# A fifth landing buffer and a reordered first block in a one-core two-block kernel

## The chip, the cores and the metric

The kernel is one program on one core of a Trainium2 chip. The metric is device time in microseconds (us), taken as the median over several executions. Before the change it was 1045.44 us, the median of 3 runs (1043.22 to 1045.67). The engines are called PE (TensorE, matrix products), ACT (ScalarE), DVE (VectorE), POOL (GpSimd) and SP (SyncE, which here only issues transfers).

## The reference

256 tokens of 1024 features pass through a first block (a modulated convolution module and a squared-ReLU network) and then through two layers of a second block (attention mixers and a gated network). The change touches only the head of the first block:

```python
mod = silu(c) @ w_mod + b_mod                  # 6 parts of 1024: sh1, s1, g1, sh2, s2, g2
h   = rms_norm(x, norm1_g) * (1 + s1) + sh1
u   = h @ w_pw1 + b_pw1                        # 1024 -> 2048
a, gate = split(u)
u   = a * sigmoid(gate)
u   = dwconv(u, w_dw) + b_dw                   # width 31, inside segments of 64 tokens
u   = silu(layer_norm(u))
x   = x + g1 * (u @ w_pw2 + b_pw2)
# then the squared-ReLU network, modulated with sh2, s2, g2
```

## The kernel before, in words

All arithmetic is float32. A weight matrix is read from memory in chunks of 128x1024, split into a rounded high part (`hi`, a copy on ACT, L409) and the remainder (`lo`, a subtraction on DVE, L426), and a product is three one-pass PE products of rounded operands (hi with high, lo with high, hi with low: L927 to L929 for the first matrix, `pw1`).

All weights come as one stream whose order is written out in `TRANSFERS`, and SP issues its transfers in that order, each of them 128x2048 (1.05 MB) or half of that. There are two kinds of landing buffers. Chunks that are split land in one of three `raw` buffers, two chunks to a buffer, which is free again once both `lo` subtractions are done. Pieces of the modulation matrix `w_mod` are used as they are and land in a `home`; of those there are four, in rotation, and one is free again when its user on PE or DVE is through (`W.used`). `Weights.pump` (L395) issues transfers until the next one has no buffer assigned. SP takes them strictly in order: when one waits for its buffer, everything behind it waits too.

In `TRANSFERS` and `PW1_STEPS` the names are these. `c0` to `c15` are the chunks of `pw1`. `F0` to `F3` are quarters of sh1 and s1, of two pieces each: PE multiplies them with silu(c) (L750), ACT copies the row of sums out (L760, into the tile `modrow`), eight small PE products turn it into columns (L777), and DVE adds the bias (L781). `M1` to `M3` mean that a quarter is taken up: the columns, and then the modulation of two of the eight feature groups (`modulated`, L864 to L873). `D0` to `D3` are pieces of s2, summed on DVE by two multiplications each (L788) with `czb`, which is silu(c) on all partitions: it is transferred (L881) and computed by a sigmoid on ACT (L979) and a multiplication on DVE (L981). `P0` to `P7` and `R0` to `R3` are pieces of g1, sh2 and g2, on PE (L750). `w0` to `w7` are the chunks of the next matrix, `pw2`.

`PW1_STEPS` sets the order in which all engines get the work of this stage. The 2048 columns of `pw1` are done as four parts q of 512 columns for two halves of the tokens, t. Chunks c0 to c11 serve q = 0 to 2 and c12 to c15 serve q = 3. When a part is complete, `glu` takes it: a sigmoid on ACT (L887) and a multiplication on DVE (L888) for each t. Then `conv` works on it: PE transforms (`x_ps`, L907), DVE multiplies by the transformed taps `wf` (L910), PE transforms back (`c_ps`, L914), ACT copies out (L919). The convolution's steps stand in the queues between the chunks. The eight PSUM banks are handed out in turn.

Ahead of `c0` the PE queue holds four products of a zeroed tile (`idle_ps`, L535), the bias products of q = 0 and 1 (L818, L819), quarter F0 (L750), the sum of squares over the features (`cs_ps`, L622), F0's columns (L777), the tap sums (`wf_ps`, L827), and the bias products of q = 2. The bias row and the tap rows lie in `rows1`, whose first half is later overwritten with `czb`.

Of the kernel before, what the change touches and what calls it, by code (L numbers as in the profile page):

```python
# [10 lines left out]
F32 = mybir.dt.float32  # L11
F32R = mybir.dt.float32r
# [3 lines left out]
P = 128  # L16
T = 256
D = 1024
# [14 lines left out]
PW2_EARLY, PW2_LATE = [0, 1, 2, 3], [4, 5, 6, 7]  # L33
WO_EARLY, WO_LATE = [6, 7, 3, 4], [5, 0, 1, 2]
EPS = 1e-6
WARM = 4
NEG = -1.0e30
VW = 392
LAYERS = 2
# [4 lines left out]


TRANSFERS = (
    "F0 c0 F1 c1,2 c3 F2 c4,5 F3 c6,7 D0 c8,9 D1 D2 c10,11 D3 P0 c12,13 P1 P2 P3 c14,15 P4 P5 w0,1 P6 P7 R0 w2,3 R1 R2 R3 "
    "w4,5,6,7"
)
PW1_STEPS = (  # L50
    "c0 F1 c1 M1 c2 F2 c3 c4 M2 c5 F3 c6 c7 M3 D0 c8 c9 D1 c10 D2 c11 D3 P0 c12 P1 c13 P2 c14 P3 c15"
)


# [423 lines left out]
def tile_conformer_then_mixer(ctx: ExitStack, tc: tile.TileContext, stream, xT, pT, vec, con, rows_in, taps, c_row, out):  # L478
    nc = tc.nc
    ctx.enter_context(tc.manual_schedule())  # L480
    cp = ctx.enter_context(tc.tile_pool(name="cp", bufs=1))
    rawp = ctx.enter_context(tc.tile_pool(name="rawp", bufs=RAWS))
    spp = ctx.enter_context(tc.tile_pool(name="spp", bufs=LOOK + 1))
    xsp = ctx.enter_context(tc.tile_pool(name="xsp", bufs=2))
    tp = ctx.enter_context(tc.tile_pool(name="tp", bufs=2))
# [4 lines left out]
    def bank(name):  # L490
        return pp_.tile([P, 512], F32, tag="b", name=name)

    vecs = cp.tile([P, NVEC], F32, name="vecs")
    cons = cp.tile([P, NCON], F32, name="cons")
    h = cp.tile([P, KB, T], F32, name="h")
# [4 lines left out]
    u = bigf[:, 2048 : 2048 + 2 * D].rearrange("p (t c) -> p t c", t=2)  # L500
    prods = bigf[:, 4096 : 4096 + NSEG * D].rearrange("p (s c) -> p s c", s=NSEG)
    wf = bigf[:, 8192 : 8192 + D]
    rows1 = bigf[:, 9216 : 9216 + 2 * D]
# [8 lines left out]
    homes = [  # L512
        cp.tile([P, 2048], F32, tag="pp", name="home0"), xsp.tile([P, 2048], F32, tag="cx", name="home1", bufs=1),
    ]
    pair = xsp.tile([P, 2, 2048], F32, tag="xs", name="home2")
    homes += [pair[:, 0, :], pair[:, 1, :]]
    W = Weights(nc, rawp, spp, stream, homes)
    W.pump()

    def V(name, i=0, n=None):  # L520
        off, cnt = VEC[name]
        return vecs[:, off + i : off + i + (n if n is not None else cnt - i)]

    def C(name):
        off, cnt = CON[name]
        return cons[:, off : off + cnt]
# [2 lines left out]
    epst = cp.tile([P, 1], F32, name="epst")  # L529
    nc.vector.memset(epst, EPS)  # L530

    nc.vector.memset(u[:, 0, :512], 0.0)
    idle_ps = bank("idle_ps")
    for _ in range(WARM):
        nc.tensor.matmul(idle_ps, u[:, 0, :P], u[:, 0, :512], start=True, stop=True)  # L535
    cz = cp.tile([P, KB, 32], F32, name="cz")
    nc.vector.memset(cz, 0.0)
    nc.scalar.preload_act_table_set("silu_and_others")
# [79 lines left out]
    def col_sum(*parts):  # L618

        ps = bank("cs_ps")  # L620
        for i, part in enumerate(parts):
            nc.tensor.matmul(ps[:, :T], ones, part, start=(i == 0), stop=(i == len(parts) - 1))  # L622
        return ps[:, :T]
# [115 lines left out]
    mods = cp.tile([P, 6, KB], F32, name="mods")  # L739
    mod_cols = bank("mod_cols")  # L740
    mod_ps = {}

    def mod_chunk(what, which, j):

        if j == 0:
            mod_ps[0] = bank("mod_ps")
        i, w = W.whole(("mod", what, which, j))
        for g in range(4):
            k = {"first": 4 * j + g, "pair": j, "one": 2 * j + g // 2}[what]
            nc.tensor.matmul(  # L750
                mod_ps[0][32 * g : 32 * g + 32, :], cz[:, k, :], w[:, 512 * g : 512 * g + 512],
                start=(j == 0), stop=(j == {"first": 1, "pair": KB - 1, "one": 3}[what]),
            )
        W.used(i)

    def mod_columns(what, which):


        row = tp.tile([P, 512], F32, tag="modrow", name="modrow", bufs=1)
        nc.scalar.copy(row, mod_ps[0])  # L760
        yield
        yield
        if what == "pair":
            at = lambda a: a.rearrange("p (q c b) -> p q c b", q=6, c=2)[:, which : which + 2]
            cols = at(mod_cols[:, :48])
            for b in range(4):
                nc.tensor.matmul(cols[:, :, :, b], row[:, b * P : (b + 1) * P], C("sel4"), start=True, stop=True)
        elif what == "one":
            at = lambda a: a.rearrange("p (q c b) -> p q c b", q=6, c=2)[:, which]
            cols = at(mod_cols[:, :48])  # L770
            for b in range(4):
                nc.tensor.matmul(cols[:, :, b], row[:, b * P : (b + 1) * P], C("sel2"), start=True, stop=True)
        else:
            at = lambda a: a.rearrange("p (q k) -> p q k", q=6)[:, :2, 2 * which : 2 * which + 2]
            cols = at(mod_cols[:, :48])
            for b in range(4):
                nc.tensor.matmul(  # L777
                    cols[:, b // 2, b % 2 : b % 2 + 1], row[:, b * P : (b + 1) * P], C("sel1"), start=True, stop=True
                )
        yield  # L780
        nc.vector.tensor_add(at(mods.rearrange("p q k -> p (q k)")), cols, at(V("b_mod")))  # L781
# [29 lines left out]
    def pw1_bias(q):  # L811

        gated[q] = [bank("g_ps") for _ in range(2)]
        kw = dict(skip_group_check=True)
        s = slice(512 * q, 512 * q + 512)
        for ps in gated[q]:
            if q < 3:
                nc.tensor.matmul(ps, ones_r, b_hi[:, s], start=True, stop=False, **kw)  # L818
                nc.tensor.matmul(ps, ones_r, b_lo[:, s], start=False, stop=False, **kw)  # L819
            else:  # L820
                nc.tensor.matmul(ps, ones[32:33, :], rows1[32:33, s], start=True, stop=False, **kw)

    def tap_sums():

        pss = [bank("wf_ps") for _ in range(2)]
        for c in range(2):
            nc.tensor.matmul(  # L827
                pss[c][:RANK], C("at")[:TAPS], rows1[:TAPS, 512 * c : 512 * c + 512], start=True, stop=True
            )
        yield  # L830
        for c in range(2):
            nc.scalar.copy(wf[:RANK, 512 * c : 512 * c + 512], pss[c][:RANK])

    for q in range(2):
        pw1_bias(q)
    sh = mods[:, 0, :]

    def quarter(c):
# [6 lines left out]
    def normed(k0, k1):  # L845
        for k in range(k0, k1):
            nc.vector.tensor_mul(xn[:, k, :], h[:, k, :], rbc)
# [4 lines left out]
    ps = col_sum(accA)  # L852
    rsqrt_(rbc, ps, 1.0 / D)
    normed(0, 2)
    for _ in work:
        pass
    sums = tap_sums()
    next(sums)
    pw1_bias(2)

    def modulated(c):

# [10 lines left out]
            nc.vector.tensor_sub(xs[:, k, T:], xn[:, k, :], xs[:, k, :T])  # L873

    modulated(0)
    for _ in sums:
        pass
    normed(2, KB)

    czb = rows1[:, :D]  # L880
    nc.sync.dma_start(czb, c_row.to_broadcast([P, D]))  # L881


    def glu(q):
# [88 lines left out]
    works = {}  # L973
    for item in PW1_STEPS.split():
        taken(item[0], int(item[1:]))
        if item == "c4":
            nc.sync.dma_start(cons[:, CON_FIRST:], con[:, CON_FIRST:])
        elif item == "c5":
            nc.scalar.activation(u[:, 0, :], czb, AF.Sigmoid)  # L979
        elif item == "c6":  # L980
            nc.vector.tensor_mul(czb, czb, u[:, 0, :])  # L981
        elif item == "c10":
            pTs0 = embedding(0)
# [31 lines left out]
        pass  # L1015
    nc.scalar.preload_act_table_set("silu_and_others")

    biasr = cp.tile([P, 5, 384], F32, name="biasr")
    rows = dram.tile([5, 384], F32, name="rows")
    skew = dram.tile([5, P + 1, 384], F32, name="skew")  # L1020

# [80 lines left out]
    ps = col_sum(*parts)  # L1102
# [8 lines left out]
    hi, lo = W.get(("pp", 0, 0))  # L1111
# [652 lines left out]
```

## Time and profile before

| | |
|---|---|
| median of 3 runs (lowest, highest) | 1045.44 us (1043.22, 1045.67) |
| the profiled execution | 1044.48 us |
| its span, first to last instruction | 1042.7 us |
| outside the span | 1.8 us |
| PE busy, share of the span | 1011.0 us, 97% |
| DVE, ACT, POOL busy | 753.6, 592.8, 101.6 us |
| mean granted PE clock | 0.978 |
| bytes moved | 192.90 MB, 185 GB/s over the span |

A line of a timeline gives the start, the time from start to end, engine, source line, operation, output and inputs by the program's names (all large work tiles are views of one tile, `big`), shape, a count where equal neighbours are merged, and in brackets the idle time of the engine before it with what ended it. `[9.31 <-DVE big L888]` says that the engine stood idle for 9.31 us until a DVE instruction of line 888 was done. A float32 product appears as several PE records. PEclk is the clock granted to PE, 1.00 being the full one.

### The profile page before, as it was taken

To read this page: it belongs to the slowest core of one execution; us is meant where nothing else is said; L and a number is where in the kernel's file an instruction comes from. 1 tells how busy PE (TensorE), PEld (TensorE's weight loads), DVE (VectorE), ACT (ScalarE), POOL (GpSimd) and SP (SyncE) were. 2 spreads that over 40 slices of the span, in tenths; PEclk is the share of its full clock that TensorE was granted. 3 is DMA by queue.
4 is the path that set the end of the run, shared out by engine and by line. 5 is a ranking of instruction groups with operands and counts; after the bars stand their busy time and mean duration, and the time that the engine had idled before them with its cause. 6 is when DMAs were issued, how large, how long until landed. Compare 5 with 4: busy or idle time off the path is not lost.

```text
span 1042.7 us, 16472 instructions
## 1 busy us (share of the span) xinstructions
PE 1011.0 (97%) x6394; PEld 870.1 (83%) x6394; DVE 753.6 (72%) x1446; ACT 592.8 (57%) x1072; POOL 101.6 (10%) x86
## 2 busy tenths in 40 slices
PE   9987989999999999999999999999999999999996
PEld 4653579888888988988888888998989888888896
DVE  5463456966878699868888865477997788886645
ACT  5522574744555554767555544674586756555455
POOL 0000022000004000002000002610000200000243
PEclk7987999999999999999999999999999999999999
DMA  9965838455554532425545555454343455555541
GB/s 376 408 235 226 338 112 267 171 202 180 186 188 160 198 125 93 162 96 188 192 174 201 177 187 195 154 172 157 107 152 122 153 197 179 199 196 174 196 162 41
DMA packets 28416, 192.90 MB, mean 185 GB/s; under 512 B 3368, under 2 KB 3757, under 8 KB 6961
## 3 DMA queue, kind: packets, MB, share of 16 engines
q1 hardware_dynamic: 26784, 188.32, 50.2%
q0 software_dynamic: 784, 1.99, 0.7%
q10 hardware_dynamic: 770, 1.54, 0.4%
q8 instruction: 50, 0.82, 0.3%
q14 instruction: 28, 0.23, 0.1%
HBM read 190.78 MB, written 2.04 MB: 185 GB/s over the span
## 4 chain that ended last, share of the span: by engine, by line
PE 78%; DVE 8%; ACT 4%; DMA 1%; issue 1%; DVEq 0%; ACTq 0%
PE g_ps L644 33%; PE g_ps L645 17%; PE g_ps L637 3%; PE mx_ps L706 3%; PE g_ps L638 2%; PE g_ps L639 2%; PE mx_ps L707 2%; PE mx_ps L708 2%; DVE lo L426 2%; DMA home<-stream 1%; ACT hi L409 1%; PE mod_ps L750 1%; PE o_ps L1423 1%; PE cs_ps L622 1%; PE pt_ps L1460 1%
## 5 line engine op out<-in xcount | busy, mean ns | idle before, releaser
L409 ACT CAST hi<-raw 128x1024 fp32r<-128x1024 f32 (+2 forms) x310 | 320.5, 1037 | 294.7 <-PE g_ps L644 148.7
L426 DVE TENSOR_TENSOR lo<-raw,hi 128x1024 fp32r<-128x1024 f32 (+2 forms) x294 | 361.0, 1231 | 125.3 <-ACT hi L409 124.4
L644 PE MATMUL g_ps<-xf,hi 128*128 128x512 f32 x704 | 247.0, 395 | 0.0
L645 PE MATMUL g_ps<-xf,lo 128*128 128x256 f32 x704 | 197.4, 280 | 0.0
L644 PEld LDWEIGHTS g_ps<-xf,hi 128*128 128x128 f32 x704 | 132.0, 187 | 30.8
L645 PEld LDWEIGHTS g_ps<-xf,lo 128*128 128x128 f32 x704 | 133.0, 189 | 0.1
L644 PE MATMUL g_ps<-big_f,hi 128*128 128x512 f32 x352 | 124.4, 397 | 0.0
L645 PE MATMUL g_ps<-big_f,lo 128*128 128x256 f32 x352 | 99.1, 281 | 0.0
L644 PE MATMUL g_ps<-big,hi 128*128 128x512 f32 x256 | 90.5, 397 | 0.0
L644 PEld LDWEIGHTS g_ps<-big_f,hi 128*128 128x128 f32 x352 | 66.1, 188 | 16.3
L645 PE MATMUL g_ps<-big,lo 128*128 128x256 f32 x256 | 72.1, 282 | 0.0
L644 PE MATMUL g_ps<-xs_h,hi 128*128 128x512 f32 x192 | 67.0, 393 | 0.0
L645 PEld LDWEIGHTS g_ps<-big_f,lo 128*128 128x128 f32 x352 | 66.4, 189 | 0.0
L644 PEld LDWEIGHTS g_ps<-big,hi 128*128 128x128 f32 x256 | 48.1, 188 | 11.8
L645 PE MATMUL g_ps<-xs_h,lo 128*128 128x256 f32 x192 | 53.8, 280 | 0.0
L608 POOL TENSOR_TENSOR accP<-accP,sq 128x256 f32<-128x256 f32 x12 | 17.8, 1480 | 331.1 <-ACT sq L607 331.1
L645 PEld LDWEIGHTS g_ps<-big,lo 128*128 128x128 f32 x256 | 48.3, 189 | 0.1
L644 PEld LDWEIGHTS g_ps<-xs_h,hi 128*128 128x128 f32 x192 | 36.0, 187 | 8.1
L637 PE MATMUL g_ps<-xs_l,hi 128*128 128x256 f32 x144 | 42.3, 294 | 0.0
L638 PE MATMUL g_ps<-xs_l,lo 128*128 128x256 f32 x144 | 41.2, 286 | 0.7 <-DVE lo L426 0.7
L637 PE MATMUL g_ps<-xn,hi 128*128 128x256 f32 x144 | 41.8, 290 | 0.0
L639 PE MATMUL g_ps<-xs_l,hi 128*128 128x256 f32 x144 | 41.0, 285 | 0.0
(363 smaller groups left out, 2238.5 us busy)
## 6 DMA issues: line engine op xcount, KB each, us to landing
raw<-stream SPq DMA_DIRECT2D x142, 1024.0 KB, 4.8
home<-stream SPq DMA_DIRECT2D x24, 1024.0 KB, 8.4
raw<-stream SPq DMA_DIRECT2D x4, 904.0 KB, 4.7
raw<-stream SPq DMA_DIRECT2D x4, 768.0 KB, 4.3
raw<-stream SPq DMA_DIRECT2D x2, 896.0 KB, 4.4
raw<-stream SPq DMA_DIRECT2D x2, 784.0 KB, 4.8
h<-xT SPq DMA_DIRECT2D x1, 1024.0 KB, 6.5
raw<-stream SPq DMA_DIRECT2D x2, 512.0 KB, 11.2
```

The lines of the kernel that those rows point to most:

```text
L409: self.nc.scalar.copy(hi[:, : PLAN[i][1]], raw)
L426: eng.tensor_sub(lo[:, :w], raw, hi[:, :w])
L608: nc.gpsimd.tensor_add(acc, acc, s)
L622: nc.tensor.matmul(ps[:, :T], ones, part, start=(i == 0), stop=(i == len(parts) - 1))
L637: nc.tensor.matmul(ps, hi, xs[:, k, :T], start=first, stop=False)
L638: nc.tensor.matmul(ps, lo, xs[:, k, :T], start=False, stop=False)
L639: nc.tensor.matmul(ps, hi, xs[:, k, T:], start=False, stop=last)
L644: nc.tensor.matmul(ps, hi, xs[:, k, :], start=first, stop=False, skip_group_check=True)
L645: nc.tensor.matmul(ps[:, :T], lo, xs[:, k, :T], start=False, stop=last, skip_group_check=True)
L706: nc.tensor.matmul(ps, hi[:, s], xs[:, k, :T], start=first and m < 4, stop=False, **kw)
L707: nc.tensor.matmul(ps, lo[:, s], xs[:, k, :T], start=False, stop=False, **kw)
L708: nc.tensor.matmul(ps, hi[:, s], xs[:, k, T:], start=False, stop=last, **kw)
```

## The change

A fifth home, `bias_home`, is added (128x2048 float32); the second block's table `biasr`, which had a tile of its own, becomes a view of it. The order strings change: `c14,15` is transferred ahead of `P3`; the quarters F2 and F3 are multiplied ahead of `c2` and `c4`, and the dots D0 to D3 start two to three chunks sooner; M3 moves from after `c7` to ahead of it. The rows of sums of the quarters no longer share one `modrow` tile but alternate between two halves of `u`. The tap sums, with ACT's copies of them, move ahead of F0. The transfer of `c_row` follows them directly, and czb's sigmoid and multiplication are tied to `c2` and `c3` in place of `c5` and `c6`. The transfer of the second part of the constants is tied to `c5` in place of `c4`. The four products of zeros become fourteen one-pass products, 432 columns wide, of a rounded copy of the constants, and four more of them stand after the bias products of q = 2, ahead of c0. The copy takes one of the three `lo` buffers until these are done.

```diff
-WARM = 4
+WARM = 14
 TRANSFERS = (
-    "F0 c0 F1 c1,2 c3 F2 c4,5 F3 c6,7 D0 c8,9 D1 D2 c10,11 D3 P0 c12,13 P1 P2 P3 c14,15 P4 P5 w0,1 P6 P7 R0 w2,3 R1 R2 R3 "
+    "F0 c0 F1 c1,2 c3 F2 c4,5 F3 c6,7 D0 c8,9 D1 D2 c10,11 D3 P0 c12,13 P1 P2 c14,15 P3 P4 w0,1 P5 P6 P7 R0 w2,3 R1 R2 R3 "
     "w4,5,6,7"
 PW1_STEPS = (
-    "c0 F1 c1 M1 c2 F2 c3 c4 M2 c5 F3 c6 c7 M3 D0 c8 c9 D1 c10 D2 c11 D3 P0 c12 P1 c13 P2 c14 P3 c15"
+    "c0 F1 c1 M1 F2 c2 c3 F3 c4 M2 D0 c5 c6 D1 M3 c7 D2 c8 c9 D3 c10 P0 c11 P1 c12 P2 c13 c14 P3 c15"
...
+    bias_home = cp.tile([P, 2048], F32, name="home4")
     pair = xsp.tile([P, 2, 2048], F32, tag="xs", name="home2")
-    homes += [pair[:, 0, :], pair[:, 1, :]]
+    homes += [pair[:, 0, :], pair[:, 1, :], bias_home]
...
-    nc.vector.memset(u[:, 0, :512], 0.0)
-    idle_ps = bank("idle_ps")
-    for _ in range(WARM):
-        nc.tensor.matmul(idle_ps, u[:, 0, :P], u[:, 0, :512], start=True, stop=True)
+    spare = spp.tile([P, 1024], F32R, tag="lo", name="spare")
+    nc.vector.tensor_copy(spare[:, :432], cons[:, :432])
+    def spare_products(n):
+        ps = bank("spare_ps")
+        for _ in range(n):
+            nc.tensor.matmul(
+                ps[:, :432], spare[:, 432 - P : 432], spare[:, :432], start=True, stop=True
+            )
...
-        row = tp.tile([P, 512], F32, tag="modrow", name="modrow", bufs=1)
+        rows_at[0] = 512 - rows_at[0]
+        row = u[:, 1, rows_at[0] : rows_at[0] + 512]
...
-    for q in range(2):
-        pw1_bias(q)
+    spare_products(WARM)
+    czb = rows1[:, :D]
+    for c in range(2):
+        pw1_bias(c)
+    tap_sums()
+    nc.sync.dma_start(czb, c_row.to_broadcast([P, D]))
...
-    sums = tap_sums()
-    next(sums)
     pw1_bias(2)
+    spare_products(4)
...
     modulated(0)
-    for _ in sums:
-        pass
     normed(2, KB)
-    czb = rows1[:, :D]
-    nc.sync.dma_start(czb, c_row.to_broadcast([P, D]))
...
-        if item == "c4":
+        if item == "c5":
             nc.sync.dma_start(cons[:, CON_FIRST:], con[:, CON_FIRST:])
-        elif item == "c5":
+        elif item == "c2":
             nc.scalar.activation(u[:, 0, :], czb, AF.Sigmoid)
-        elif item == "c6":
+        elif item == "c3":
             nc.vector.tensor_mul(czb, czb, u[:, 0, :])
...
-    biasr = cp.tile([P, 5, 384], F32, name="biasr")
+    biasr = bias_home[:, : 5 * 384].rearrange("p (h c) -> p h c", h=5)
```

First, SP's queue in the second half of `pw1`. In the kernel before these are, in this order, P0 (`home_91`), c12,13 (`raw_435`), P1 (`home_92`), P2 and P3 (`home_93`), c14,15 (`raw_527`), P4, P5, and w0,1 (`raw_575`):

```order
L395 DMA home_91<-stream 128x2048
L395 DMA raw_435<-stream 128x2048
L395 DMA home_92<-stream 128x2048
L395 DMA home_93<-stream 128x2048 x2
L395 DMA raw_527<-stream 128x2048
L395 DMA home_91<-stream 128x2048
L395 DMA home_92<-stream 128x2048
L395 DMA raw_575<-stream 128x2048
```

After the change these are D3 (`home_92`), P0 (`home_94`), c12,13 (`raw_403`), P1 (`home_94`), the constants, P2 (`home_93`, the new buffer), c14,15 (`raw_454`), P3 (`home_91`), P4 (`home_92`), and w0,1 (`raw_497`):

```order
L395 DMA home_92<-stream 128x2048
L395 DMA home_94<-stream 128x2048
L395 DMA raw_403<-stream 128x2048
L395 DMA home_94<-stream 128x2048
L984 DMA cons<-con 128x1664
L395 DMA home_93<-stream 128x2048
L395 DMA raw_454<-stream 128x2048
L395 DMA home_91<-stream 128x2048
L395 DMA home_92<-stream 128x2048
L395 DMA raw_497<-stream 128x2048
```

Before, P1, P2 and P3 stand between c12,13 and c14,15, and they reuse the homes of D1, D2 and D3. Now P1, the constants and P2 stand there, and P1 and P2 reuse the homes of D0 and D1.

Second, PE's queue ahead of `c0`. Before, behind the products of zeros and eight bias products, with F0 in `home_91` and `home_92`:

```order
L750 MATMUL mod_ps<-home_91,cz 32x512 x4
L750 MATMUL mod_ps<-home_92,cz 32x512 x4
L622 MATMUL cs_ps<-accA,cons 128x256
L777 MATMUL mod_cols<-cons,modrow 128x1 x4
L827 MATMUL wf_ps<-big_84,cons 118x512 x2
L818 MATMUL g_ps<-xs_h_90 128x512
L819 MATMUL g_ps<-xs_h_90 128x512
L818 MATMUL g_ps<-xs_h_90 128x512
L819 MATMUL g_ps<-xs_h_90 128x512
L927 MATMUL g_ps<-hi_159,xs_h_90 128x512
```

After, behind the fourteen products of constants and the same eight bias products (L934 is c0's first product):

```order
L836 MATMUL wf_ps<-big_84,cons 118x512 x2
L758 MATMUL mod_ps<-home_91,cz 32x512 x4
L758 MATMUL mod_ps<-home_92,cz 32x512 x4
L629 MATMUL cs_ps<-accA,cons 128x256
L786 MATMUL mod_cols<-cons,big_84 128x1 x4
L827 MATMUL g_ps<-xs_h_90 128x512
L828 MATMUL g_ps<-xs_h_90 128x512
L827 MATMUL g_ps<-xs_h_90 128x512
L828 MATMUL g_ps<-xs_h_90 128x512
L539 MATMUL spare_ps<-spare 128x432 x4
L934 MATMUL g_ps<-hi_179,xs_h_90 128x512
```

The tap sums have gone from between F0's columns and the bias products to ahead of F0, and four products of constants stand where c0 began.

Third, DVE's queue at the first dot, D0. Before (`home_91`, line 788), with the modulation M3 ahead of it and the `lo` parts of c10 and c11 behind:

```order
L873 TENSOR_TENSOR xs_h_90<-big_84,xs_h_90 128x256 x2
L788 SCALAR_TENSOR_TENSOR home_91,mods<-home_91,big_84 128x1024 x2
L426 TENSOR_TENSOR lo_451<-raw_378,hi_437 128x1024
L426 TENSOR_TENSOR lo_467<-raw_378,hi_453 128x1024
L888 TENSOR_TENSOR big_84<-g_ps,sg 128x256
```

After (`home_94`, line 797), with M2 ahead of it and the `lo` parts of c7 and c8 behind:

```order
L885 TENSOR_TENSOR xs_h_90<-big_84,xs_h_90 128x256 x2
L797 SCALAR_TENSOR_TENSOR home_94,mods<-home_94,big_84 128x1024 x2
L426 TENSOR_TENSOR lo_401<-raw_259,hi_387 128x1024
L426 TENSOR_TENSOR lo_421<-raw_283,hi_407 128x1024
L797 SCALAR_TENSOR_TENSOR home_93,mods<-home_93,big_84 128x1024 x2
```

D0 stands three chunks earlier in DVE's queue, and `lo` parts of earlier chunks now stand behind it.

More of the change, by code (lines that the diff above doesn't have):

```diff
@@ L741, in tile_conformer_then_mixer @@
     mod_ps = {}
+    rows_at = [0]
     def mod_chunk(what, which, j):
@@ L829, in tap_sums @@
             )
-        yield
         for c in range(2):
             nc.scalar.copy(wf[:RANK, 512 * c : 512 * c + 512], pss[c][:RANK])
-    for q in range(2):
-        pw1_bias(q)
+    spare_products(WARM)
[4 more added lines that the diff above has]
+    nc.sync.dma_start(czb, c_row.to_broadcast([P, D]))
     sh = mods[:, 0, :]
```

## The prediction

> **What bounds the kernel now.** I read the page first, then the table of stretches, then the timelines of the stretch that stands out, and last SP's own queue.
>
> ```profile
> span 1042.7 us, 16472 instructions
> PE 1011.0 (97%) x6394; PEld 870.1 (83%) x6394; DVE 753.6 (72%) x1446; ACT 592.8 (57%) x1072; POOL 101.6 (10%) x86
> ```
>
> PE is the bound as a whole. What can still be gained is where PE stands idle, or is busy at half its clock. The stretches of the first block (columns: PE, PEld, DVE, ACT and POOL busy, granted PE clock, DMA share, GB/s):
>
> ```profile
> 10.50:24.10 13.60, 12.66 (x41) 6.58 (x34) 6.81 (x19) 7.41 (x12) 0.00 (x0) 0.50 1.02 420
> 24.10:60.00 35.90, 35.38 (x188) 25.00 (x187) 19.26 (x29) 18.89 (x27) 0.00 (x0) 1.00 0.88 359
> 60.00:70.00 10.00, 9.42 (x36) 5.24 (x37) 6.03 (x10) 3.09 (x6) 0.00 (x0) 0.93 0.88 338
> 70.00:80.00 10.00, 5.89 (x12) 2.56 (x11) 5.87 (x11) 0.00 (x0) 0.00 (x0) 0.67 0.61 211
> 80.00:92.40 12.40, 7.20 (x17) 2.98 (x18) 5.08 (x7) 2.37 (x3) 0.00 (x0) 0.50 0.40 168
> 92.40:115.00 22.60, 22.37 (x124) 9.80 (x123) 9.68 (x22) 7.20 (x13) 0.00 (x0) 1.00 0.68 244
> ```
>
> Between 70 and 92 us PE is idle, the clock is halved, and at the same time the DMA rate falls from 420 to 168 GB/s. So the transfers don't run out of rate: they are not issued. The same with cuts at c0's first product, at the end of c11 and at the end of P7 (PE busy, clock, DMA share, GB/s):
>
> ```profile
> 21.07:65.38 44.31, 43.79 (x217) 0.97 0.90 367
> 65.38:114.93 49.55, 39.49 (x165) 0.79 0.60 222
> ```
>
> Why PE stands, followed backwards: PE, DVE and ACT.
>
> ```profile
> 74.39 1.50 PE L907 MATMUL x_ps<-big,cons 64*118 64x512 f32 x2
> 85.20 2.05 PE L907 MATMUL x_ps<-big,cons 64*118 64x512 f32 x2 [9.31 <-DVE big L888]
> 87.19 0.79 PE L927 MATMUL g_ps<-hi,xs_h 128*128 128x512 f32 x1
> ```
>
> ```profile
> 75.78 0.08 DVE L788 DVE_READ_ACCUMULATOR home<-home,big 128x1 f32 x1
> 84.72 0.42 DVE L888 TENSOR_TENSOR big<-g_ps,sg 128x256 f32<-128x256 f32 x1 [8.85 <-ACT sg L887]
> 85.06 1.22 DVE L426 TENSOR_TENSOR lo<-raw,hi 128x1024 fp32r<-128x1024 f32 x1
> ```
>
> ```profile
> 83.36 1.04 ACT L409 CAST hi<-raw 128x1024 fp32r<-128x1024 f32 x1 [14.03 <-DMA raw<-stream]
> 84.31 0.38 ACT L887 ACTIVATE sg<-g_ps 128x256 f32<-128x256 f32 x1
> ```
>
> The last transform pair waits for a `glu` multiplication, this for a sigmoid, and the sigmoid stands on ACT behind the `hi` copy of c14, which waits 14.03 us for c14,15 to land. SP's queue says when that was issued:
>
> ```profile
> 58.77 0.33 SPq L395 DMA_DIRECT2D home<-stream  x1
> 59.15 0.43 SPq L395 DMA_DIRECT2D raw<-stream  x1
> 63.66 12.57 SPq L395 DMA_DIRECT2D home<-stream  x3
> 76.32 0.38 SPq L395 DMA_DIRECT2D raw<-stream  x1
> ```
>
> These are P0, c12,13, then P1 to P3, then c14,15 at 76.32. P3 reuses D3's home, and DVE is done with D3 at 75.86 (the read of the accumulator above). So the chain is: the fourth dot, P3's issue, c14,15 behind it, ACT, DVE, PE.
>
> **What the stretch is worth.** From 65.38 to 114.93 PE idles 49.55 - 39.49 = 10.1 us. The half clock costs half of PE's busy time under it: 7.20/2 = 3.6 in 80 to 92.4, some 2.7 in 70 to 80 (clock 0.67, so 6.6 us of it at half, of which 5.3 busy), and 0.7 before 70: 7.0. With 0.5 of idle time ahead of 65.38 that is 17.6 us, the most that this edit can bring here.
>
> **The change, part by part.** *Fifth home, sooner dots, c14,15 ahead of P3.* What lies ahead of c14,15 now waits for D1's dot, not D3's, and the dots stand two to three chunks sooner. If SP never stops, landings follow each other at the rate of 10.5 to 24.1 us, 420 GB/s, or 2.5 us per 1.05 MB. F0's second piece has landed when PE goes on at 12.56:
>
> ```profile
> 12.56 1.94 PE L750 MATMUL mod_ps<-home,cz 128*32 128x512 f32 x8 [0.94 <-DMA home<-stream]
> 14.42 1.22 PE L622 MATMUL cs_ps<-accA,cons 128*128 128x256 f32 x2
> 15.44 1.82 PE L777 MATMUL mod_cols<-cons,modrow 128*128 128x1 f32 x8
> ...
> 18.19 2.76 PE L827 MATMUL wf_ps<-big,cons 31*118 31x512 f32 x3
> ...
> 21.07 0.80 PE L927 MATMUL g_ps<-hi,xs_h 128*128 128x512 f32 x1
> ```
>
> From there to c14,15 the order string has 21 pieces of 1.05 MB, and by their shapes `c_row` and the constants are about 1.3 more: 22.3 x 2.5 = 56, so it lands at about 68.5, or 69 with the small `pT` transfer. The buffers it passes come free in time: D1's dot at about 52, c9's `lo` part at about 57 (PE places, from the chunk spacing below), both more than 10 us ahead of that. PE needs it when the last transform pair stands, after the first half of c12. With c0 starting at 23.3 (below): 43.8 of work as between 21.07 and 65.38, two P pieces of 1.0 each (half of 12.56's 1.94), bias products 1.9, half a chunk 1.4: 72.4. The margin is some 3 us, the closest of this change. The later transfers have more, since P3 to P7 land by 84 and are used from 88 on. So the 17.6 go, and the next thing due is PE's own work.
>
> *Tap sums and spare products first.* This moves work ahead of c0. One dense product of 512 columns starts every 0.43 us at half clock and every 0.23 at full:
>
> ```profile
> 22.52 0.63 PE L927 MATMUL g_ps<-hi,xs_h 128*128 128x512 f32 x1
> 22.94 0.63 PE L928 MATMUL g_ps<-lo,xs_h 128*128 128x512 f32 x1
> ...
> 24.66 0.39 PE L927 MATMUL g_ps<-hi,xs_h 128*128 128x512 f32 x1
> 24.89 0.39 PE L928 MATMUL g_ps<-lo,xs_h 128*128 128x512 f32 x1
> ```
>
> So a spare product (432 columns) is 0.36 or 0.19. They wait for the constants and for a copy on DVE:
>
> ```profile
> 3.78 0.22 DVE L798 CAST xs_h<-cons 1x128 fp32r<-1x128 f32 x1 [2.07 <-DMA cons<-con]
> ```
>
> The copy is about 0.5 (432/1024 of 1.22, L426), so PE starts at 4.3, where the products of zeros began at 1.49 and needed no data:
>
> ```profile
> 1.49 6.46 PE L535 MATMUL idle_ps<-big 128*128 128x512 f32 x8 [1.49 <-DVE big L532]
> ...
> 8.22 0.39 PE L819 MATMUL g_ps<-xs_h 1*128 1x512 f32 x1
> ```
>
> Fourteen at half clock end at 9.4. Eight bias products take 3.4 at half, 1.9 at full clock; the tap sums 3.4 or 1.7 (2.76 for three of four records at half); F0 3.9 or 2.0. All halved: 9.4 + 3.4 + 3.4 + 3.9 = 20.1, where F0 ended at 14.5 before. At full clock from the middle of the spare products on, 14.2, just behind F0's landing. I take 17.5, since the table shows 0.50 all through 10.5 to 24.1 although PE was busy for 12.66 of the 13.60, so full clock is not to be counted on there. Then as before: ACT's copy 0.8, columns 1.8, bias products of q = 2 1.7, four spare ones 1.5: c0 starts at 23.3 against 21.07, a loss of 2.2 (ends: -1.5, as F3's second piece, at 37, then holds c4 back; and 25.9, +4.8). c0's own clock rises somewhat later: 0 to 1.7, taken as 0.5. Nothing hides this, since PE is without a gap from c0 on.
>
> The Trainium skill ("TensorE: Matmul & The Clock Gate", Part 1) says that one busy window of about 3.4 us lifts the gate; by that the spare products alone would lift it in half of all cases, and c0 would start near 21, giving 1028. This trace speaks against counting on it: in the row 80 to 92.4 PE is busy for 7.20 us without a gap and the clock stays at 0.50 to the end.
>
> *The rest.* F2 and F3 sooner, `modrow` in two places, M3 sooner: the same instructions in another order; what they wait for has landed (F2 by 29, F3 by 37, from the count above; PE comes to them at about 32 and 40). `biasr` in the new home is written after P7 is used; nothing waits. `czb` is ready before D0 lands at about 42. I take 0, up to 1 as loss.
>
> *Sum.* 17.6 - 2.2 - 0.5 - 0.4 = 14.5 off the profiled 1044.48: **1030.0 us**. The median of the runs is 1045.44, within 1.0 of that.
>
> **Rivals.**
> 1. *The spare products never lift the clock before c0.* All of the head at half clock, c0 at 25.9 and 1.7 of late rise: 17.6 - 6.5 - 0.4 = 10.7, 1033.8. For it: 0.50 in the whole first row of the table. Against: the zeros did lift it: the bias product at 8.22 took 0.39, as a product of the same width does at full clock. Chance 0.12.
> 2. *c14,15 lands late and some of the stall stays.* It decides from 72.5 on, 1 us for 1. At the 359 GB/s of 24 to 60 us, 2.92 per piece, it lands at 78.4: 5.9 lost, 1035.9. Against: that row's 0.88 is a DMA share with gaps, and the row before has 420. Chance 0.08. The Trainium skill ("DMA: Bandwidth & Descriptors", Specifications) gives about 358 GB/s as what HBM lends one core; by it this rival would be the forecast. The first row, at 420, does not agree with it.
> 3. *It is given back at R0 to R3.* R0 waits for P3, R1 to R3 for P4 to P6, so they still come in a bunch; one more piece in the bunch is 2.5, two 5: 1032.5 to 1035. Before, this wait was small:
>
> ```profile
> 126.56 0.64 PE L750 MATMUL mod_ps<-home,cz 128*32 128x512 f32 x4 [0.23 <-DMA home<-stream]
> ```
>
> Chance 0.05.
>
> 4. *Slower: DVE's queue blocks where SP's did.* D0 stands ahead of the `lo` parts of c7 and c8 now. If its transfer lands late, DVE waits, c7 waits, and the raw buffers behind them too. It decides from about 47, when PE is through with M2, 1 us for 1; for the whole to be slower D0 must land after 47 + 14.5 = 61 instead of 42. For it: a dot that DVE takes late is what holds SP now. Against: 0.88 of the DMA share up to 60 us. At 65, 1048. Chance 0.04.
> 5. *No change*: the rate really falls after 60 us, and no issue order helps. Within 1044.5 +- 3. Against: SP issues only three transfers in the 12.57 us from 63.66 on, and a rate falls when nothing is asked for. Chance 0.03.
>
> **How the numbers follow.** The forecast has the remaining 0.68; its own range is 1026 (c0 at 19.6) to 1033. The range of 8 in 10 takes in the first two rivals: 1026 to 1037. The smallest difference that a measurement of this kernel tells from no change is about 0.3%, 3.1 us. Faster: 0.68 + 0.12 + 0.08 + 0.05 = 0.93; within: 0.03; slower: 0.04.
>
> **What would show it.** Right: SP issues c14,15 before 60 us; the hi copy of c14 no longer waits for 14 us; no wait of PE for L888's successor near 72; clock 1.00 from the end of c0 to P7; P7 ends at about 100 (114.93 - 14.5); after that all timelines are the old ones, shifted. Wrong: c0's first product after 26 or before 20, a PE wait of over 2 us between c0 and P7, a half clock in there, or a wait over 1 us ahead of R0 to R3.

## The result and the profile after

The changed kernel takes **1028.21 us** (median of 4 runs, 1027.14 to 1029.32) beside 1045.41 for the kernel before, run in turns on the same chip: a ratio of 0.984, 95% interval 0.9821 to 0.986, or some 17 us. The forecast was 1030.0 with a range of 1026 to 1037. The profiled execution took 1029.32 us, its span 1027.5, so 15.2 us less than the span of before.

The page of after, its head. PE is busy for 10 us less, with ten records more: the products run at a higher clock.

```profile
span 1027.5 us, 16494 instructions
PE 1001.0 (97%) x6404; PEld 870.1 (85%) x6404; DVE 753.5 (73%) x1446; ACT 593.0 (58%) x1072; POOL 101.6 (10%) x86
```

The table of stretches, with the columns as before (PE, PEld, DVE, ACT, POOL busy, granted clock, DMA share, GB/s):

```profile
10.50:24.10 13.60, 12.28 (x62) 6.96 (x63) 8.82 (x21) 7.29 (x13) 0.00 (x0) 0.87 1.01 418
24.10:60.00 35.90, 33.42 (x174) 23.74 (x166) 21.86 (x35) 19.16 (x28) 0.00 (x0) 1.00 1.01 420
60.00:70.00 10.00, 10.00 (x45) 5.52 (x46) 7.27 (x12) 3.27 (x7) 0.00 (x0) 1.00 1.02 418
70.00:80.00 10.00, 10.00 (x47) 4.68 (x46) 6.04 (x9) 3.48 (x5) 0.00 (x0) 1.00 1.01 421
```

The hole between 70 and 92 us is gone: PE is busy without a gap at full clock from 60 to 80, and the transfers run on at 418 to 421 GB/s where they had fallen to 211 and 168. SP's queue and the `hi` copy of c14 on ACT show the two ends of the chain:

```profile
52.02 0.33 SPq L395 DMA_DIRECT2D home<-stream  x1
56.51 0.33 SPq L395 DMA_DIRECT2D raw<-stream  x1
58.80 5.22 SPq L395 DMA_DIRECT2D home<-stream  x2
```

```profile
69.93 1.05 ACT L409 CAST hi<-raw 128x1024 fp32r<-128x1024 f32 x1 [3.49 <-DMA raw<-stream]
70.89 0.38 ACT L894 ACTIVATE sg<-g_ps 128x256 f32<-128x256 f32 x1
```

```profile
71.30 0.42 DVE L895 TENSOR_TENSOR big<-g_ps,sg 128x256 f32<-128x256 f32 x1 [4.03 <-ACT sg L894]
```

```profile
71.13 1.98 PE L914 MATMUL x_ps<-big,cons 64*118 64x512 f32 x8
```

c14,15 is issued at 56.51 (before 76.32) and has landed by 69.93 (before 83.36). The sigmoid is 13.4 us sooner, and the last transform pair on PE, which had stood for 9.31 us, stands no more. It is just in time: the `glu` multiplication ends at 71.72, and the last pair starts at 72.09, behind the others of its group (the eight records from 71.13). By the kernel's text this transform reads the columns of q = 0 and 1, while the multiplication is of q = 2. So what it waits for is hardly data; a PSUM bank that comes free with the multiplication is likely, but no run gave it another bank. Nor was the sigmoid put ahead of c14's `hi` copy, which would cut the same chain. From c0's first product to the end of P7, after first and then before:

```profile
19.34:97.17 77.83, 75.18 (x381) 44.90 (x379) 47.84 (x82) 33.95 (x51) 0.00 (x0) 0.99 0.93 382
```

```profile
21.07:114.93 93.86, 83.28 (x381) 48.03 (x380) 48.74 (x84) 33.95 (x52) 0.00 (x0) 0.87 0.75 290
```

The same 381 products take 16.03 us less. Idle time falls from 93.86 - 83.28 = 10.58 to 77.83 - 75.18 = 2.65, which is 7.93; busy time falls by 8.10, and that is the clock (0.87 to 0.99). c0 itself starts 1.73 us sooner, so P7 ends 17.76 us sooner.

The head, PE's timeline of after:

```profile
4.18 4.43 PE L539 MATMUL spare_ps<-spare 128*128 128x432 f32 x14 [4.18 <-DVE spare L534]
8.54 0.49 PE L827 MATMUL g_ps<-xs_h 1*128 1x512 f32 x1
...
10.54 1.02 PE L836 MATMUL wf_ps<-big,cons 31*118 31x512 f32 x2
11.48 1.06 PE L758 MATMUL mod_ps<-home,cz 128*32 128x512 f32 x8
12.73 1.07 PE L758 MATMUL mod_ps<-home,cz 128*32 128x512 f32 x8 [0.18 <-DMA home<-stream]
13.73 0.70 PE L629 MATMUL cs_ps<-accA,cons 128*128 128x256 f32 x2
15.56 1.05 PE L786 MATMUL mod_cols<-cons,big 128*128 128x1 f32 x8 [1.14 <-ACT big L769]
...
19.34 0.63 PE L934 MATMUL g_ps<-hi,xs_h 128*128 128x512 f32 x1
```

The spare products end at 8.6, not 9.4, and all that follows them up to F0 runs at full clock: F0's halves take 1.06 each, where the second took 1.94 before. F0 waits for its landing for only 0.18 us and ends at 13.8. The tap sums stand in the time in which PE had waited for F0.

**Given back behind P7.** From the end of P7 to the end of the span, before needs 927.8 us and after 930.4: P7 ends 17.76 us sooner, the span only 15.2. PE has the same 5965 records there and stands idle about as long (18.6 and 18.4 us), but it is busy for 911.9 us where before has 909.1. The difference is in the clock: after runs at half of it in four windows of 3.4 us,

```profile
99.51:102.91 3.40, 3.40 (x15) 1.41 (x15) 1.10 (x4) 2.52 (x7) 0.00 (x0) 0.51 1.01 414
137.02:140.43 3.41, 3.41 (x13) 3.06 (x14) 2.45 (x5) 2.65 (x7) 2.44 (x5) 0.50 0.26 64
399.80:403.20 3.40, 3.40 (x16) 3.22 (x16) 2.83 (x12) 1.78 (x7) 0.00 (x0) 0.50 0.02 5
676.30:679.70 3.40, 3.40 (x13) 3.40 (x12) 1.07 (x2) 1.89 (x5) 0.00 (x0) 0.50 1.00 352
```

and before in two (all ahead of the drain at the end):

```profile
153.90:157.30 3.40, 3.40 (x14) 3.05 (x14) 2.65 (x6) 2.74 (x7) 2.56 (x5) 0.50 0.28 73
416.70:420.10 3.40, 3.40 (x16) 3.23 (x16) 2.80 (x13) 1.95 (x8) 0.00 (x0) 0.50 0.17 24
```

A window costs half of the busy time in it, 1.7 us. Two more of them are 3.4, and 2.6 were given back; the 0.8 between wasn't traced.

### The profile page after: what moved, and what is told of

It reads as the page before. It is cut to its first block, busy times and chain, and to the rows that moved or that the text cites. A ratio compares the mean times of both kernels' runs of the same rounds, so it can differ in the third digit from the quotient of the medians.

```text
span 1027.5 us, 16494 instructions
## 1 busy us (share of the span) xinstructions
PE 1001.0 (97%) x6404; PEld 870.1 (85%) x6404; DVE 753.5 (73%) x1446; ACT 593.0 (58%) x1072; POOL 101.6 (10%) x86
## 4 chain that ended last, share of the span: by engine, by line
PE 82%; DVE 9%; ACT 5%; DMA 3%; issue 1%; SPq 0%; DVEq 0%; ACTq 0%
PE g_ps L651 34%; PE g_ps L652 17%; PE mx_ps L713 3%; PE g_ps L644 3%; DMA home<-stream 3%; PE mx_ps L714 3%; PE mx_ps L715 3%; PE g_ps L645 3%; PE g_ps L646 2%; DVE lo L426 2%; PE mod_ps L758 1%; ACT hi L409 1%; PE g_ps L934 1%; PE cs_ps L629 1%; PE o_ps L1430 1%
```

## The experiments

The theory: SP's queue held c14,15 behind P3's home, and the gain is that stretch. The rivals on its parts: the fifth home alone frees the queue; the new order alone frees it; the new head is needed, or costs time; the second row of sums is for nothing. The sooner dots with neither the home nor the swap weren't run. In the table, "c0" is the start of c0's first product and "P7" the end of P7, both in the profiled execution; "rest" is the span behind P7. The ratio is to the kernel before, timed on the same chip in turns.

| kernel | c0 | P7 | rest | ratio, 95% interval |
|---|---|---|---|---|
| before | 21.07 | 114.9 | 927.8 | 1 |
| after | 19.34 | 97.2 | 930.4 | 0.984 (0.9821, 0.986) |
| swap only | 21.19 | 110.8 | 929.2 | 0.9972 (0.9954, 0.9989) |
| fifth home only | 21.32 | 108.1 | 930.0 | 0.9946 (0.9928, 0.9964) |
| new orders only | 21.36 | 105.1 | 928.2 | 0.9912 (0.9885, 0.994) |
| all but the new head | 20.58 | 102.3 | 930.2 | 0.9892 (0.9878, 0.9906) |
| after, four homes | 19.83 | 98.9 | 931.2 | 0.9845 (0.9824, 0.9867) |
| the same, one row of sums | 19.70 | 100.9 | 935.1 | 0.9892 (0.9875, 0.9908) |
| after, P3 first | 19.43 | 99.4 | 930.3 | 0.9864 (0.9843, 0.9886) |
| after, tap sums late | 23.87 | 101.6 | 928.9 | 0.9886 (0.9849, 0.9922) |
| after, no spare products | 20.56 | 100.2 | 928.7 | 0.9864 (0.9827, 0.99) |
| after, zeros for constants | 21.28 | 98.6 | 932.7 | 0.9853 (0.9822, 0.9884) |
| after, M3 back | 19.81 | 97.2 | 928.8 | 0.9851 (0.9827, 0.9874) |
| after, gaps filled | 18.09 | 97.1 | 927.8 | 0.9828 (0.981, 0.9847) |

**Only c14,15 ahead of P3** (the kernel before with the new `TRANSFERS`):

```diff
-... P0 c12,13 P1 P2 P3 c14,15 P4 P5 w0,1 P6 P7 R0 ...
+... P0 c12,13 P1 P2 c14,15 P3 P4 w0,1 P5 P6 P7 R0 ...
```

> The kernel before with the transfer string alone changed (c14,15 ahead of P3, P5 behind w0,1). Queue theory: c14,15 now waits behind P2, which waits for D2's dot (over at 71.8 in the trace of before), so it is issued at 72 instead of 76, lands at 79 instead of 83, and PE's stall ahead of the last transform pair falls from 9.3 to about 5: 1040 to 1042. If only the position behind P3 had been the cause: 1030. Theory of the head: 1045.

1041.57 us, within what was expected. P2 still waits for D2's home, so c14,15 moves by one dot only: it is issued at 72.9, and its `hi` copy waits for 10.13 us where it had waited for 14.03:

```profile
80.19 1.04 ACT L409 CAST hi<-raw 128x1024 fp32r<-128x1024 f32 x1 [10.13 <-DMA raw<-stream]
```

**Only the fifth home**, with the rows of sums in `u`, since their tile's room is taken:

```diff
-    homes += [pair[:, 0, :], pair[:, 1, :]]
+    homes += [pair[:, 0, :], pair[:, 1, :], bias_home]
-        row = tp.tile([P, 512], F32, tag="modrow", name="modrow", bufs=1)
+        row = u[:, 1, rows_at[0] : rows_at[0] + 512]
```

> The kernel before with the fifth home alone (and the rows of sums in u, which makes room for it); both order strings, the tap sums and the products of zeros stay as they were. Queue theory: P3 now reuses D2's home, not D3's, and c12,13 comes behind P0 in F3's home, which is free at about 47 us; DVE then never waits on ACT's copy of c12, so D2's dot is done at about 64 instead of 72, SP issues c14,15 at about 65 and it lands at about 70: most of the 9.3 us stall goes, 1029 to 1032. Theory of the head (the gain came from the sooner start of c0 and its clock): no change, 1044 to 1046. Theory that the home helps only together with the new order: 1041 (P3's wait moves from D3's to D2's dot, 4 us).

1040.19 us: the queue theory missed by some 10 us, and the value named for a home that helps only with the new order, 1041, came near. The dots still stand late in DVE's queue, and a buffer more doesn't bring them forward. From 60 to 70 us DVE is busy without a gap, where before had 6.03 of the 10:

```profile
60.00:70.00 10.00, 9.46 (x40) 5.69 (x39) 10.00 (x18) 3.81 (x7) 0.00 (x0) 1.00 0.74 244
70.00:80.00 10.00, 4.55 (x14) 1.90 (x13) 5.00 (x9) 1.33 (x2) 0.00 (x0) 0.75 0.97 351
```

c14,15 is issued at 69.6, and PE's transform pair still waits:

```profile
78.76 2.05 PE L910 MATMUL x_ps<-big,cons 64*118 64x512 f32 x2 [5.45 <-DVE big L891]
```

**Only the new orders**, with four homes, one row of sums and the old head:

```diff
 TRANSFERS, PW1_STEPS: as after the change
-        if item == "c4":
+        if item == "c5":
             nc.sync.dma_start(cons[:, CON_FIRST:], con[:, CON_FIRST:])
-        elif item == "c5":
+        elif item == "c2":
-        elif item == "c6":
+        elif item == "c3":
```

> The kernel before with the new order strings (and czb's work tied to c2 and c3) but four homes; head as before. Queue theory: the dots of D0 to D2 are through at about 46, 52 and 58, so P0, P1 and P2 find their homes free and c14,15 is issued before 60 and lands at 70: 1029 to 1032 without any fifth home. Theory that the fifth buffer is what counts: SP still stops behind P1 or P2, c14,15 lands after 75, 1036 to 1042. Theory of the head: 1044 to 1046.

1035.08 us (1033.43 to 1039.70), 3 above what was expected. The hole is gone with four homes too: c14's `hi` copy stands at 73.05 with 0.29 us of wait, on PE. What is lost lies ahead of it: F3's row must wait until M2's columns have read the only `modrow`, and the `hi` copies behind it on ACT wait with it.

```profile
45.00 0.59 ACT L760 COPY modrow<-mod_ps 128x512 f32<-128x512 f32 x1 [6.11 <-PE mod_cols L777]
45.48 1.05 ACT L409 CAST hi<-raw 128x1024 fp32r<-128x1024 f32 x1
```

**After with four homes**, and then **with one row of sums as well**:

```diff
-    homes += [pair[:, 0, :], pair[:, 1, :], bias_home]
+    homes += [pair[:, 0, :], pair[:, 1, :]]
# the second kernel also (biasr is a tile of its own again, too):
-        row = u[:, 1, rows_at[0] : rows_at[0] + 512]
+        row = tp.tile([P, 512], F32, tag="modrow", name="modrow", bufs=1)
```

> The changed kernel with four homes. Queue theory with sooner dots: P0, P1 and P2 reuse the homes of D0, D1 and D2, whose dots are over at 46, 52 and 59; c14,15 is issued at about 60 and lands at 70 as before: 1028 to 1030, no more than 2 us lost. Theory that the fifth buffer is what counts: c14,15 lands after 75 and the transform pair waits 4 us or more: over 1032.

> The changed kernel with four homes and with the rows of sums in one modrow tile again (the kernel with four homes and two rows came to 1030.48, 0.9845 of before). In the new order F3 is multiplied before F2's row is taken up as M2. Theory that the second row is what the new order needs: ACT's copy of F3's row waits about 6 us for M2's columns, as it did with the new orders on the old kernel; the hi copy of c6 and M2 stand behind it, PE loses 4 to 6 us between c5 and c9, 1034 to 1037. Theory that the row's place costs nothing, as predicted: 1029 to 1031.

1030.48 us, ratio 0.9845: with the sooner dots the fifth home is worth nothing that can be measured (P7 is 1.7 us later, a window at half clock at 57.4). With one row, 1035.19 us and 0.9892: the second row is needed. Its trace shows the mechanism, the same wait as above:

```profile
42.47 0.59 ACT L766 COPY modrow<-mod_ps 128x512 f32<-128x512 f32 x1 [5.90 <-PE mod_cols L783]
```

```profile
46.65 0.50 PE L931 MATMUL g_ps<-hi,xs_h 128*128 128x512 f32 x1 [1.39 <-ACT xs_h L881]
51.49 0.50 PE L932 MATMUL g_ps<-lo,xs_h 128*128 128x512 f32 x1 [0.68 <-DVE lo L426]
```

These two waits are 2.1 us of PE's time, and P7 ends 2.0 us later than with two rows. The profiled execution loses another 3.9 us behind P7, of which 3.4 are two more windows at half clock (6.8 us at 404 and 3.4 at 684, against 3.4 at 402 alone with two rows). That these follow from the row isn't shown, so of the timed 0.0047, some 4.9 us, only 2.1 are.

**After with P3 ahead of c14,15** (the old `TRANSFERS`, nothing else):

> The changed kernel with the transfer string of before (P3 ahead of c14,15 again). Queue theory: P3 reuses D2's home, whose dot is over at about 59, so SP no longer stops there; c14,15 lands one piece later, 72.4 instead of 69.9, and PE, which came to the last transform pair at about 71 and waited for nothing, now waits 1 to 2 us: 1029 to 1031. If the place ahead of P3 is what matters: the stall of 9.3 us is back, 1040.

1032.41 us, 1.4 above what was expected; the interval overlaps that of after. c14,15 is issued at 59.8, and its `hi` copy stands at 72.34, as forecast. That is late: the weights of the last transform wait for the `glu` multiplication, and the group of eight takes 2.73 us where after has 1.98.

```profile
72.56 2.73 PE L914 MATMUL x_ps<-big,cons 64*118 64x512 f32 x8
74.18 0.28 PEld L914 LDWEIGHTS x_ps<-big,cons 64*118 64x118 f32 x2 [0.48 <-DVE big L895]
```

The 0.75 between is the price of the landing, less than the 1 to 2 us that were expected, and that although PE comes to the group 1.4 us later than in after. P7 ends 2.2 us later, with 1.7 of it in a window at half clock at 57.0. So the stall of 9.3 us stays away without the swap, and in time the swap is worth nothing that is clear of the scatter.

**All but the new head** (the new orders, five homes and two rows, on the kernel before):

> The kernel before with the fifth home, the two rows and both order strings; tap sums, c_row's transfer and the products of zeros as before. Theory that the queue's part is 17.6 and the head takes some of it back (as predicted): 1027 to 1029, not slower than the changed kernel. Theory that the new head helps (c0 at 19.3 instead of 21.1, and full clock 3 us sooner): c0 at 21.3, full clock at 25, no stall at c14, 1031 to 1034.

1036.02 us, ratio 0.9892 (0.9878 to 0.9906), clear of after and above what either theory gave. The prediction's loss in the head is refuted: as part of the whole change the new head is worth some 5 us. PE's timeline shows two waits for F0 that the tap sums now fill, and one behind the late ones:

```profile
10.17 1.07 PE L752 MATMUL mod_ps<-home,cz 128*32 128x512 f32 x8 [0.77 <-DMA home<-stream]
12.68 1.93 PE L752 MATMUL mod_ps<-home,cz 128*32 128x512 f32 x8 [1.44 <-DMA home<-stream]
...
17.20 1.45 PE L830 MATMUL wf_ps<-big,cons 31*118 31x512 f32 x3
19.43 0.79 PE L821 MATMUL g_ps<-xs_h 1*128 1x512 f32 x1 [0.79 <-ACT big L835]
```

c0 starts 1.24 us later for that. The other 3.9 us up to P7 are clock:

```profile
20.58:102.33 81.75, 79.79 (x381) 48.06 (x380) 48.64 (x84) 33.67 (x51) 0.00 (x0) 0.92 0.88 358
```

The same 381 products are busy for 79.79 where after has 75.18. How much of that is the head's doing isn't settled: a window at 60.3 and one at 73.9, far behind the head, come to 3.4 of it at 1.7 each.

**After with the tap sums late** (`tap_sums` and `c_row` back in their old places, spare products kept; ACT's copies of the sums follow directly, where before has them behind the first modulation):

```diff
-    tap_sums()
-    nc.sync.dma_start(czb, c_row.to_broadcast([P, D]))
...
+    tap_sums()                 # behind modulated's columns, ahead of pw1_bias(2)
...
+    nc.sync.dma_start(czb, c_row.to_broadcast([P, D]))   # after normed(2, KB)
```

> The changed kernel with the tap sums back between F0's columns and the bias products of q = 2, and the transfer of c_row back behind the first modulation. If moving them made the sooner start of c0: c0 begins 1.5 to 3.5 us later (four records of 0.5 to 0.85), at 21 to 23; c_row no longer stands ahead of F2's second piece, so PE waits about 1 us less for F2 and F3, and the sum is 0 to 2 slower, 1028 to 1030. If the move was of no use: c0 at 19.3.

1034.74 us, some 5 above what was expected. In the trace c0 starts 4.5 us later and P7 ends 4.4 later; the timed intervals just overlap. Of the 4.5, PE waits 0.49 for one of ACT's copies. With the taps late the spare products don't help: the old head, which has late taps and no spare products, has c0 at 20.58, 3.3 us sooner than here. Without the taps between bias and F0 the clock falls at 12.5 and stays down until 26.2,

```profile
10.50:26.20 15.70, 14.44 (x49) 8.03 (x48) 7.35 (x20) 7.76 (x14) 0.00 (x0) 0.57 1.02 421
```

and the taps cost their time twice, at half clock and on the path:

```profile
17.84 1.20 PE L836 MATMUL wf_ps<-big,cons 31*118 31x512 f32 x1
...
18.83 2.76 PE L836 MATMUL wf_ps<-big,cons 31*118 31x512 f32 x3
```

**After without the spare products**, and **with four products of zeros for the first fourteen**:

```diff
-    spare_products(WARM)
# the first kernel also:
-    spare_products(4)
# the second, where the spare tile was made:
+    nc.vector.memset(u[:, 0, :512], 0.0)
+    idle_ps = bank("idle_ps")
+    for _ in range(4):
+        nc.tensor.matmul(idle_ps, u[:, 0, :P], u[:, 0, :512], start=True, stop=True)
```

> The changed kernel without any of the eighteen spare products (the copy of the constants stays). If they lift the clock: PE starts with the bias products at about 7.4 us at half clock, F0 ends at about 18, c0 starts at 22 to 24 instead of 19.3 at half clock, and since PE waits 2.5 us for transfers between 24 and 60 anyway, about 1 to 3 us are lost: 1029 to 1031. If they are of no use (the head waits for F0's landing and for the columns anyway): c0 at 19 to 20, 1027 to 1029. Theory of the head as the main cause: most of the 17 us are lost, over 1038.

> The changed kernel with the four products of zeros of before in place of the fourteen spare products (the four spare products ahead of c0 stay). If what counts is that PE is busy, whatever the data: zeros from 1.5 to 7.9 us lift the clock at about the same time, c0 at 19 to 20.5, 1027 to 1029. If zeros do less for the clock than rounded constants: the clock falls back before F0 is through, c0 at 21 to 23, 1028.5 to 1031.

1031.19 and 1032.67 us (the latter from 1027.74 to 1033.05), both intervals overlapping after's; the first is at the upper end of what was expected, the second 1.7 above it. In the traces c0 starts 1.2 and 1.9 us later, and P7 ends 3.0 and 1.4 later; of the 3.0, 1.7 is a window at half clock at 58.9. So what the spare products are worth isn't clear of the scatter, in c0 it is less than the tap sums' place, and whether rounded constants raise the clock better than zeros stays open.

**What is left.** Between c0 and P7 after has 2.2 us of waits in the chunks behind M3's modulation, and then 1.28 behind P7:

```profile
55.28 0.49 PE L934 MATMUL g_ps<-hi,xs_h 128*128 128x512 f32 x1 [1.04 <-ACT hi L409]
56.54 0.50 PE L935 MATMUL g_ps<-lo,xs_h 128*128 128x512 f32 x1 [0.77 <-DVE lo L426]
59.97 0.50 PE L935 MATMUL g_ps<-lo,xs_h 128*128 128x512 f32 x1 [0.42 <-DVE lo L426]
```

Two kernels go for these: **M3 back behind c7**, and **gaps filled**, which also copies F0's row on ACT ahead of c0's `hi` copy, transfers the second part of the constants after c11, and puts one more product behind P7, into a bank that nothing reads:

```diff
-    "... D0 c5 c6 D1 M3 c7 D2 c8 ..."
+    "... D0 c5 c6 D1 c7 M3 D2 c8 ..."
# the second kernel also:
+    work = quarter(0)          # moved ahead of c0's hi copy
-        if item == "c5":
+        if item == "c11":
             nc.sync.dma_start(cons[:, CON_FIRST:], con[:, CON_FIRST:])
+    fill_ps = bank("fill_ps")  # behind P7
+    nc.tensor.matmul(fill_ps[:, :432], ones, cons[:, :432], start=True, stop=True)
```

> The changed kernel with M3 behind c7 again. In the changed kernel PE stands 1.0 and 0.8 us at 54 to 57 us, because ACT's hi copy of the next chunk stands behind M3's modulation. If that is M3's place: those two gaps go, c11 ends 1.8 us sooner, and what is then left is decided by c14,15, which lands at 70: of 1.8 us between 0.5 and 1.8 are gained, 1026 to 1028. If the gaps are from the transfers: no change, 1027 to 1029.

> The changed kernel with M3 behind c7, the second part of the constants transferred after c11 (so c14,15 lands 2 us sooner), F0's row copied on ACT ahead of c0's hi copy, and one product of the constants on PE behind P7, where PE stands 1.3 us and the clock was at half for 3.4 us behind it. If the remaining gaps are worth what the trace shows: 1.1 for the row, 1.8 for M3, and up to 1.5 for the clock behind P7: 2 to 4 us faster than the changed kernel, 1024 to 1026. If c14,15 or the clock's free windows decide: within 1 of the changed kernel.

Ratios 0.9851 and 0.9828, beside 0.984 for after: neither is clear of it. The median of the first, 1032.12 us (1027.96 to 1034.41), is 3 above what was expected of either theory, and the 2 to 4 us expected of the second weren't seen. P7 ends at 97.2 and 97.1, as in after: the waits of about 2 us only move to other chunks, and in the second kernel the 1.25 us by which c0 is sooner go to a half clock up to 24.2. Behind P7 the second has none of after's four windows at half clock until 1021,

```profile
97.11:102.90 5.79, 5.44 (x36) 3.46 (x36) 3.04 (x9) 4.83 (x11) 0.00 (x0) 1.00 0.93 362
136.90:140.40 3.50, 3.50 (x29) 3.33 (x29) 3.32 (x6) 2.98 (x7) 2.36 (x5) 1.00 0.65 139
```

and its profiled execution is the shortest of all, 1026.76 us; its five runs reach up to 1031.21.

## Why the prediction was right, and where it was wrong

- **The stretch: right.** 17.6 us were to go, less 0.5 for a late clock. From c0 to P7 it was 16.0. Both kinds of loss went, in other shares than forecast: 7.9 of idle time where 10.6 had been put, and 8.1 of clock where it was 7.0 less the late clock's 0.5. (That term was a gain: from c0 on after runs at half clock for 1.6 us, before for 3.1.) The chain of waits was the right one, but it had more than one remedy: the swap alone is worth 2.9 us, the home alone 5.6, the orders alone 9.2 (one less the ratio, times 1045). In the whole change either the home or the swap can be left out without a loss that is clear of the runs' scatter; the parts don't add up, since they cut the same wait. What stands in every kernel without the hole is the sooner dots; whether they would do it alone wasn't run.
- **c14,15 at 69: right; a margin of some 3 us: wrong.** It had landed by 69.93. But the forecast set the landing against PE's transform pair and left out what lies between: the `hi` copy, the sigmoid and the multiplication, 1.79 us from 69.93 to 71.72. The last pair starts at 72.09, so the margin was 0.4 at most, and the kernel with P3 first has used it up. That there was any is luck: counted on from the real c0, the prediction's sum has PE at the pairs at 68.4, and PE came at 71.13, with 2.5 us of waits between 24 and 60 us that the forecast didn't have. The rate held at 418 to 421 GB/s, so rival 2 falls. The Trainium skill ("DMA: Bandwidth & Descriptors", Specifications) gives about 358 GB/s; this trace doesn't agree with it as a limit for this one core.
- **The head: wrong, in sign.** The step was "moves work ahead of c0", with F0's end at 17.5 and c0 at 23.3. F0 ended at 13.8 and c0 began at 19.34, beyond the better end of the range that was given (-1.5), and "before 20" stands in the prediction among the signs of being wrong. Of the 4.0 us, 3.7 lie ahead of F0's end, and the step that failed is the clock there: half the head was put at half clock, since the table showed 0.50 there before; with the taps in between, the clock stays full until 17.5. The case of full clock had been worked out as 14.2 (its terms, 4.3 + 7 x 0.36 + 7 x 0.19 + 1.9 + 1.7 + 2.0, give 13.75) and was set aside. Besides, the tap sums were added to the path, though PE had a wait for F0 there (0.94 us in the row quoted, 0.77 and 1.44 in the kernel with the old head) that they fill. The prediction's estimate by the Trainium skill ("TensorE: Matmul & The Clock Gate", Part 1), that one busy window of about 3.4 us lifts the gate, was c0 near 21 and 1028, nearer to both than its forecast. The rise in after agrees roughly: the spare products start every 0.36 us up to 7.23 and every 0.20 from 7.47 on, so the clock rose at about 7.3, 3.1 us behind the first of them. The 13.6 us at half clock that before had, with PE busy for 12.66 of them, don't agree.
- **"The rest", 0.4 and at most 1: too small.** 2.65 us of idle time stay between c0 and P7, most of them in the chunks behind M3, which now stands sooner. And "`modrow` in two places" was no side matter: without the second row PE waits for 2.1 us more.
- **Behind P7 "the old ones, shifted": wrong** by the 2.6 us given back. So the sum came out near by errors that cancel: the head was better by 1.7 + 2.2 = 3.9 us, the stretch less by 17.6 - 0.5 - 0.4 - 16.0 = 0.7, and what follows P7 worse by 2.6: 14.5 + 3.9 - 0.7 - 2.6 = 15.1, the span's difference.
- **The rivals.** 1 (no rise of the clock), 2 (a late landing), 3 (R0 to R3 in a bunch; PE shows no wait ahead of them) and 5 didn't happen. 4 didn't in the whole change, but its resource was the bound elsewhere: in the kernel with the fifth home only, DVE is full from 60 to 70 us.

## What to carry to other kernels

When a queue that issues in strict order stands for a buffer, look at the place of the buffer's last consumer in its own queue. Here the orders alone brought 9.2 us and one more buffer alone 5.6, and together with the new orders the buffer brought nothing that the runs show. When a landing is set against the moment at which PE needs it, add the steps between. When a step is taken up sooner, look for the single scratch tile behind it: here the one row of sums would have cost a part of the gain. And small work that needs no stream data may go into the wait for the first landing; look for such a wait before pricing the work as added to the path.

## What the runs showed of the hardware that was not expected

- **The clock moves on a grid.** In every trace PE's clock changes at multiples of 3.41 us from one another, and a window at half clock often follows a short wait: in after, 1.14 us of idle time at 14.4 and 1.28 behind P7 were enough. But the gap behind P7 is 1.27 us in before too (the first row below), and there the clock stays full until 153.9. How the grid cuts the gap doesn't explain it: in both kernels the gap lies whole in one step of the grid, with PE busy for 2.13 of 3.41 us (96.05 to 99.46 in after, 112.90 to 116.31 in before). For the waits behind M3's modulation the cut does go with the fall. The waits of 1.04 and 0.77 us come in one step in the kernels with four homes, with P3 first, without spare products and with the old head: PE is busy there for 1.62 to 1.67 us, and the next step is at half clock. In after they come in two steps, busy for 2.57 and 2.46, and the clock stays full. So 1.7 us of these kernels' later P7 goes with where the grid lay. Nor is idle time needed for a fall: in the kernel with the old head PE is busy without a gap from 70.53 to 73.94, and the next step is at half clock. Likewise, in the kernel with the gaps filled, PE is busy for 3.33 of 3.41 us, with one-column and one-row products among others, and the next two windows are at half clock (the two rows below that, with the columns of the stretches).

```profile
116.21 1.05 PE L767 MATMUL mod_cols<-cons,modrow 128*128 128x4 f32 x8 [1.27 <-ACT modrow L760]
```

```profile
13.96:17.37 3.41, 3.33 (x18) 2.30 (x16) 2.09 (x5) 2.05 (x4) 0.00 (x0) 1.00 1.02 423
17.37:24.20 6.83, 6.22 (x17) 3.85 (x20) 5.48 (x13) 3.09 (x4) 0.00 (x0) 0.51 1.00 410
```

A window is worth 1.7 us of PE's time, so an edit that should gain less than 2 us can't be judged by one execution of this kernel. What exactly the clock counts wasn't settled.

- **One stage has two paces.** In the large gated products of the second block PE is busy without a gap at full clock, and yet 100 us hold either 568 or 579 products, 2%. After has the faster pace in the first layer and the slower one in the second,

```profile
473.00:573.00 100.00, 100.00 (x579) 88.17 (x578) 85.62 (x146) 58.51 (x108) 0.00 (x0) 1.00 0.53 190
823.00:923.00 100.00, 100.00 (x568) 86.75 (x567) 83.79 (x144) 57.23 (x106) 0.00 (x0) 1.00 0.54 188
```

before the other way round, and the kernel with gaps filled the slower one in both (567 and 569). A layer's stage, 704 products from the first start to the last, takes 122.84 or 125.12 us. The 2.3 us between cancel between before and after, and they are part of the scatter of "rest" in the table: the kernel with the new orders only has the faster pace in both layers, those with the swap only, with the fifth home only and with four homes the slower one in both. The cause isn't known.
